# Operands in two parts for the next-state products of a state-space branch, and its B by C products taken for four token blocks at once, in a hybrid decoder trunk on one Trainium2 core

## The chip, the cores and the metric

The kernel runs on one core of one Trainium2 chip. The metric is device time in microseconds (us), the median of the runs. Lower is better. Engines are named as in the profile: PE is TensorE (matrix products, PEld its weight loads), DVE is VectorE, ACT is ScalarE, POOL is GpSimd, SP issues the loads and stores.

## The reference, cut to what matters

One decoder layer is computed for 512 tokens of width 1024 in float32: a norm, one wide projection, three mixing branches (dilated attention, pooling, a state-space branch), gates, an output projection, then a gated convolutional feed-forward part and a last norm. The change lies in the state-space branch, which goes over the tokens in four blocks of 128:

```python
xc = (x * dt[..., None]).reshape(b, c, l, g, e, p)
a_cs = jnp.cumsum(a, axis=-1)
Lmat = jnp.exp(jnp.where(causal, seg, -jnp.inf)).reshape(b, g, e, c, l, l)
cb = jnp.einsum("bclgn,bcsgn->bcgls", Cc, Bc)
y_diag = jnp.einsum("bcgls,bgecls,bcsgep->bclgep", cb, Lmat, xc)
decay = jnp.exp(a_cs[..., -1:] - a_cs).reshape(b, g, e, c, l)
states = jnp.einsum("bclgn,bgecl,bclgep->bcgepn", Bc, decay, xc)
def step(carry, inp):
    st, dec = inp
    return carry * dec[..., None, None] + st, carry
```

`y_off` takes C by the state carried into a block, and the branch's output is `y_diag + y_off`. There are two groups `g` of eight heads, a state of 128, and 64 channels a head.

## The kernel before, in words

**Stages.** The weights come in jobs of 256 columns or so. A job is loaded by SP (`raw`, in `fetch`), split by ScalarE into a high part in fp32r (`wh`, line 196) and by VectorE into the rest (`wl = raw - wh`, line 216), two jobs ahead of its use. TensorE then takes three fp32r products for each chunk (`mm3`, line 237): high by high, high by low, low by high. Each chunk collects in a PSUM bank (`pa`, `pqk`, `pu`, `pb`) and is then evacuated.

**The order of the work.** Each engine executes its instructions in the order in which the program writes them (`manual_schedule`). The big products follow a written list (`program`, `jobs`). The small work of attention and of the state-space branch stands in generators. After each chunk `step()` lets every running generator go on to its next `yield`; `ROWS`, `WHOLE` and `REST` order what they give TensorE within a step. So between two chunks of 24 long products (12, where `chunk_a2` halves a chunk) TensorE gets a few short ones.

**The state-space branch.** `ssd_start` queues `btok_item` for both groups, then `ssd_item(c, gi)` for block `c` and group `gi` in the order of `SSD_ORDER`, one new item at every other step. It runs beside the q and k products of the third attention group (`pqk`) and the gates (`pa`), from about 366 to 492 us.

- `btok_item` (lines 989 to 994) turns B (`XS[8 + gi]`) block by block with four transposes into the bank `pbt`, and ScalarE copies it to `btok`, in float32.
- `ssd_item` (lines 996 to 1071) first has SP load `al`, the cumulated decay spread over 128 partitions, and `ea`. It turns four blocks of x into `pxs` (line 1014); VectorE multiplies by dt into `xc` (1016). TensorE takes B by C of the block into `pcb` (line 1020), a plain float32 product of 128 columns, and VectorE masks it with a triangle into `cbt` (1022). GpSimd multiplies `xc` by the decay into `xd` (1025), for the first three blocks.
- One step on, VectorE subtracts in `al` head by head (1031) and ScalarE takes the exponentials (1032). One further, VectorE multiplies `al` by `cbt` (1036).
- Then comes the state: GpSimd scales the old one (1042), TensorE takes the product of `btok` and `xd` into `pst` (line 1045), a plain float32 product of 512 columns, and VectorE adds it (1050); in the first block ScalarE copies it (1048).
- Then `py` (1057, `xc` by `al`), `pyo` (1064, old state by C, four plain products), and VectorE's sums into the output (1066, 1067, 1070).

A plain float32 product appears in the trace as two records, an fp32r product as one.

**Buffers.** All the small PSUM banks (`SM`: `pbt`, `pxs`, `pcb`, `pst`, `py`, `pyo` and attention's `ps`, `pt`, `po`) share one ring of four, so each new one waits until an older one has been read. The SBUF tiles of `T` share a ring of 54. SP's queue is in order: weight loads, `al` and `ea` stand in it one behind the other.

Of the kernel before, what the change touches and what calls it, by code (L numbers as in the profile page):

```python
# [10 lines left out]
F32 = mybir.dt.float32  # L11
F32R = mybir.dt.float32r
AF = mybir.ActivationFunctionType
OP = mybir.AluOpType
AX = mybir.AxisListType

P = 128
# [66 lines left out]
def trunk(ctx: ExitStack, tc, out, x, rel_bias, ln1_g, w_in, b_gate, w_a, pool_w, pool_scale, w_b,  # L84
# [3 lines left out]
    act, dve, pool, pe, sp = nc.scalar, nc.vector, nc.gpsimd, nc.tensor, nc.sync  # L88
# [19 lines left out]
    def T(name, dt=F32, shape=(P, S)):  # L108
        return big.tile(list(shape), dt, name=name, tag="t")
# [4 lines left out]
    def SM(name):  # L114
        return psum.tile([P, S], F32, name=name, tag="sm")
# [5 lines left out]
    tri = cpool.tile([P, P], F32, name="tri")  # L121
# [27 lines left out]
    ROWS, WHOLE, REST = 1, 2, 3  # L149
# [744 lines left out]
    XS, YT, Y = {}, {}, {}  # L894
# [85 lines left out]
    def hb(t, c, h0, n=8):  # L980
        return t[:, c * SH + h0:c * SH + h0 + n].unsqueeze(2).to_broadcast([P, n, DH])

    def h3(t):
        return t.rearrange("p (h d) -> p h d", h=8)

    btok, prev, done = {}, {}, set()

    def btok_item(gi):
        yield WHOLE
        ps = SM("pbt")  # L990
        for c in range(4):
            pe.transpose(ps[:, c * P:(c + 1) * P], XS[8 + gi][:, c * P:(c + 1) * P], eye)
        t = btok[gi] = T("btok")
        act.copy(t, ps)

    def ssd_item(c, gi):
        cs = slice(c * P, (c + 1) * P)
        dtv, acs, dec, tot, ad, ed = (cst[n] for n in ("dtv", "acs", "dtz", "dts", "ad", "ed"))
        als = []
        for q in range(2):  # L1000
            al = T("al")
            h0 = 8 * gi + 4 * q
            sp.dma_start(al.rearrange("p (h l) -> p h l", h=4), ad[h0:h0 + 4, cs].partition_broadcast(P))
            als.append(al)
        if c:
            ea = T("ea")
            for i in range(2):
                h0 = 8 * gi + i
                sp.dma_start(ea[DH * i:DH * i + DH].rearrange("p (j l) -> p j l", j=4),
                             ed[h0:h0 + 8 - i:2, cs].partition_broadcast(DH))  # L1010
        yield WHOLE
        ps = SM("pxs")
        for j in range(4):
            pe.transpose(ps[:, j * P:(j + 1) * P], XS[4 * gi + j][:, cs], eye)
        xc = T("xc")
        dve.tensor_tensor(h3(xc), h3(ps), hb(dtv, c, 8 * gi), OP.mult)

        y = Y[gi][:, :, cs]
        pcb = SM("pcb")
        pe.matmul(pcb[:, :P], XS[8 + gi][:, cs], XS[10 + gi][:, cs], start=True, stop=True)  # L1020
        cbt = T("cbt", F32, (P, P))
        dve.tensor_tensor(cbt, pcb[:, :P], tri, OP.mult)
        if c < 3:
            xd = T("xd")
            pool.tensor_tensor(h3(xd), h3(xc), hb(dec, c, 8 * gi), OP.mult)  # L1025
        yield
        for q in range(2):
            a3 = als[q].rearrange("p (h l) -> p h l", h=4)
            for j in range(4):
                i = c * SH + 8 * gi + 4 * q + j  # L1030
                dve.tensor_scalar(a3[:, j, :], a3[:, j, :], acs[:, i:i + 1], 0.0, OP.subtract, OP.min)
            act.activation(als[q], als[q], AF.Exp)
        yield
        for q in range(2):
            a3 = als[q].rearrange("p (h l) -> p h l", h=4)
            dve.tensor_tensor(a3, a3, cbt.unsqueeze(1).to_broadcast([P, 4, P]), OP.mult)
        yield
        old = prev.get(gi)
        if c < 3:
            nw = T("st")  # L1040
            if c:
                pool.tensor_tensor(h3(nw), h3(old), hb(tot, c, 8 * gi), OP.mult)
            yield WHOLE
            pst = SM("pst")
            pe.matmul(pst, btok[gi][:, cs], xd, start=True, stop=True)
            yield REST
            if c == 0:
                act.copy(nw, pst)
            else:
                dve.tensor_tensor(nw, nw, pst, OP.add)  # L1050
            prev[gi] = nw
        yield
        py = SM("py")
        for j in range(4):
            for i in range(2):
                o, lo = (2 * j + i) * DH, (2 * j + i) % 4 * P
                pe.matmul(py[DH * i:DH * i + DH, j * P:(j + 1) * P], xc[:, o:o + DH],  # L1057
                          als[j // 2][:, lo:lo + P], start=True, stop=True)
        by_j = lambda t: t.rearrange("p (j l) -> p j l", j=4)
        yield WHOLE  # L1060
        if c:
            po = SM("pyo")
            for j in range(4):
                pe.matmul(po[:, j * P:(j + 1) * P], old[:, j * P:(j + 1) * P], XS[10 + gi][:, cs],
                          start=True, stop=True)
            dve.tensor_tensor(ea, po, ea, OP.mult)
            dve.tensor_tensor(ea, ea, py, OP.add)
        for j in range(4):
            m = 4 * gi + j
            dve.scalar_tensor_tensor(y[:, j, :], y[:, j, :], cst["dgc"][:, m:m + 1],  # L1070
                                     by_j(ea if c else py)[:, j, :], OP.mult, OP.add)
        done.add((c, gi))

    def ssd_start():
        for m in (8, 9, 0, 1, 2, 3, 10, 4, 5, 6, 7, 11):
            act.activation(XS[m], XS[m], AF.Silu)
        for gi in range(2):
            waiting.append(btok_item(gi))
        for c, gi, gap in SSD_ORDER:
            waiting.append(ssd_item(c, gi))  # L1080
            for _ in range(gap):
                waiting.append(FREE)
# [517 lines left out]
    for tb in (2, 3):  # L1600
        for h in range(2):
            t = xin[tb, h]
# [30 lines left out]
    n = 0  # L1633
# [67 lines left out]
```

## Time and profile before

| | |
|---|---|
| median of 3 runs | 1033.13 us (1032.23 to 1033.27) |
| the profiled execution: its own time | 1032.69 us |
| its span | 1030.9 us |
| TensorE busy | 1019.8 us, 5276 records |
| VectorE, ScalarE, GpSimd busy | 702.7, 490.2, 132.8 us |
| mean granted TensorE clock | 0.999 |

The time of an execution holds the span of its instructions and a little around it. Busy times of different engines lie beside one another. In the rows of a timeline the first figure is the start in us from the span's start, the second the stretch covered, then engine, line, operation, output and inputs by the program's names, shape and count; a bracket gives idle time before it and what ended it. Durations of neighbouring TensorE records overlap, so TensorE's cost is best read from start to start. In the table by stage, each engine's busy time stands with its number of instructions behind it, then the granted clock, the DMA engines' busy share and the rate moved.

### The profile page before, as it was taken

What the parts mean: (1) busy time and instruction counts of PE and PEld (TensorE: products, weight loads), DVE (VectorE), ACT (ScalarE), POOL (GpSimd) and SP (SyncE); (2) the same over time, 40 slices, a digit from 0 to 9 for tenths busy, and PEclk for the clock granted to TensorE, in tenths of its full rate; (3) what the DMA queues carried; (4) which work ended last, traced back from release to release, by engine and by line L of the source; (5) the groups of instructions that cost most, each with busy time, mean ns of one, the idle gap of its engine ahead of it and who ended that gap; (6) DMA issues with size and microseconds to landing.
All of it is one profiled execution on the core that took longest, in us unless ns stands there. A gap on an engine that the chain in (4) does not pass through costs nothing.

```text
span 1030.9 us, 13254 instructions
## 1 busy us (share of the span) xinstructions
PE 1019.8 (99%) x5276; PEld 858.0 (83%) x5276; DVE 702.7 (68%) x932; ACT 490.2 (48%) x784; POOL 132.8 (13%) x114
## 2 busy tenths in 40 slices
PE   8999999999999999999999999999999999999997
PEld 8998877899888887788888888898888888888885
DVE  6553566788756648666688856767778668685756
ACT  6432545454674363567575324545444434433434
POOL 1770000000000001100044501101111100111002
PEclk9999999999999999999999999999999999999999
DMA  8444312034322354551253625543232233421322
GB/s 270 135 129 137 108 57 75 31 88 138 123 82 82 93 158 108 133 144 44 80 151 128 203 82 203 171 142 121 82 122 83 84 117 112 138 82 41 123 82 82
DMA packets 113357, 117.62 MB, mean 114 GB/s; under 512 B 5236, under 2 KB 97207, under 8 KB 113296
## 3 DMA queue, kind: packets, MB, share of 16 engines
q1 hardware_dynamic: 112703, 115.92, 36.4%
q8 instruction: 41, 0.67, 0.3%
q10 hardware_dynamic: 592, 0.86, 0.2%
q14 instruction: 21, 0.16, 0.1%
HBM read 112.97 MB, written 2.22 MB: 112 GB/s over the span
## 4 chain that ended last, share of the span: by engine, by line
PE 91%; DVE 4%; ACT 3%; issue 1%; DMA 1%; ACTq 0%; DVEq 0%
PE pa L237 30%; PE pu L237 22%; PE pb L237 12%; PE pd L237 7%; PE pqk L237 6%; PE pa L1552 2%; PE pq L237 2%; PE pu L1356 1%; PE ps L743 1%; PE pt L772 1%; PE ppw L237 1%; PE po L784 1%; DVE xs L1133 1%; DVE wl L216 1%; PE py L1057 1%
## 5 line engine op out<-in xcount | busy, mean ns | idle before, releaser
L216 DVE TENSOR_TENSOR wl<-raw,wh 128x2048 fp32r<-128x2048 f32 (+3 forms) x95 | 220.3, 2320 | 53.3 <-ACT wh L196 43.5
L196 ACT CAST wh<-raw 128x1024 fp32r<-128x1024 f32 (+3 forms) x188 | 187.6, 1017 | 48.3 <-DVE raw L341 18.0
L1251 DVE SCALAR_TENSOR_TENSOR hc<-pu,fcol,hc 128x510 f32<-128x510 f32 x88 | 65.8, 748 | 56.0 <-ACT hc L1248 54.4
L237 PE MATMUL pa<-uh,wh 128*128 128x512 f32 x384 | 98.4, 398 | 0.0
L237 PE MATMUL pa<-ul,wh 128*128 128x512 f32 x384 | 94.9, 389 | 0.0
L237 PE MATMUL pa<-uh,wl 128*128 128x512 f32 x384 | 94.8, 389 | 0.0
L237 PEld LDWEIGHTS pa<-ul,wh 128*128 128x128 f32 x384 | 72.1, 188 | 15.1
L237 PEld LDWEIGHTS pa<-uh,wl 128*128 128x128 f32 x384 | 72.1, 188 | 15.0
L237 PE MATMUL pu<-uh,wh 128*128 128x512 f32 (+1 forms) x352 | 83.6, 379 | 0.0
L237 PE MATMUL pu<-uh,wl 128*128 128x512 f32 (+1 forms) x352 | 83.5, 379 | 0.0
L237 PE MATMUL pu<-ul,wh 128*128 128x512 f32 (+1 forms) x352 | 83.5, 379 | 0.0
L237 PEld LDWEIGHTS pa<-uh,wh 128*128 128x128 f32 x384 | 70.3, 188 | 14.8 <-issue 1.0
L237 PEld LDWEIGHTS pu<-ul,wh 128*128 128x128 f32 x352 | 64.2, 188 | 12.5
L237 PEld LDWEIGHTS pu<-uh,wl 128*128 128x128 f32 x352 | 64.2, 188 | 12.5
L237 PEld LDWEIGHTS pu<-uh,wh 128*128 128x128 f32 x352 | 64.1, 188 | 12.4
L1248 ACT ACTIVATE hc<-pu,fcol,fcol 128x512 f32<-128x512 f32 x40 | 31.2, 780 | 80.5 <-PE pu L237 80.5
L1256 POOL TENSOR_TENSOR hc<-hc 128x512 f32<-128x512 f32 x22 | 30.8, 1402 | 289.1 <-DVE hc L1251 252.0
L1025 POOL TENSOR_TENSOR xd<-xc,dtz 128x512 f32<-128x512 f32 x6 | 6.4, 1063 | 355.9 <-issue 307.5
L765 ACT ACTIVATE sb<-sb,nmls 128x128 f32<-128x128 f32 (+1 forms) x72 | 30.1, 419 | 30.4 <-DVE nmls L762 17.7
L1149 ACT ACTIVATE sg<-pa,col 128x512 f32<-128x512 f32 x24 | 16.5, 688 | 45.5 <-PE pa L237 45.4
L1253 ACT ACTIVATE hc<-hc 128x512 f32<-128x512 f32 x22 | 13.9, 632 | 39.9 <-DVE hc L1251 39.9
L907 DVE SCALAR_TENSOR_TENSOR xs<-pa,col,xs 128x509 f32<-128x509 f32 (+2 forms) x24 | 18.0, 749 | 18.7 <-ACT xs L903 18.2
(373 smaller groups left out, 1868.0 us busy)
## 6 DMA issues: line engine op xcount, KB each, us to landing
raw<-in_w_in_dram SPq DMA_DIRECT2D x25, 1024.0 KB, 5.5
raw<-in_ffn_w_up_dram SPq DMA_DIRECT2D x22, 1024.0 KB, 5.2
raw<-in_w_o_dram SPq DMA_DIRECT2D x8, 1024.0 KB, 6.6
raw<-in_ffn_w_down_dram SPq DMA_DIRECT2D x8, 1024.0 KB
raw<-in_w_in_dram SPq DMA_DIRECT2D x14, 512.0 KB, 3.9
raw<-in_w_in_dram SPq DMA_DIRECT2D x6, 768.0 KB
raw<-in_w_b_dram SPq DMA_DIRECT2D x4, 1024.0 KB, 5.2
al<-ad SPq DMA_DIRECT2D x16, 256.0 KB, 7.7
```

Source lines behind the costliest of these rows:

```text
L196: act.copy(job.high[:, :, o], job.raw[:, :, o])
L216: (eng or dve).tensor_tensor(l[:, :, o], job.raw[:, :, o], h[:, :, o].bitcast(F32), OP.subtract)
L237: pe.matmul(ps, l, r, start=first and n == 0, stop=last and n == total - 1, skip_group_check=onto)
L743: pe.matmul(pss[i][:, o:o + w * P], q[r, n * P:(n + 1) * P], k[r, kb * P:(kb + w) * P], start=True, stop=True)
L765: act.activation(sb[:, off:off + w * P], sb[:, off:off + w * P], AF.Exp, bias=nm[:, n, h:h + 1], accum_out=ls[:, n, h:h + 1])
L907: dve.scalar_tensor_tensor(t[:, sh:], ps[:, :S - sh], col[:, o_cw + 12 * k + m:o_cw + 12 * k + m + 1], t[:, sh:], OP.mult, OP.add)
L1149: act.activation(s, ps, AF.Sigmoid, bias=col[:, o:o + 1])
L1248: act.activation(t, ps, AF.Identity, bias=ff["c1"][:, ff["b"] + m:ff["b"] + m + 1], scale=fw(2, m))
L1251: dve.scalar_tensor_tensor(t[:, sh:], ps[:, :S - sh], fw(k, m), t[:, sh:], OP.mult, OP.add)
L1253: act.activation(t, t, AF.Silu)
L1256: pool.tensor_tensor(a, a, t, OP.mult)
L1552: pe.matmul(first[2 * n + j][:, lo:hi], a[:, k, j * P:(j + 1) * P], b[:, k, lo:hi], start=a is wh and b is uh and k == 0, stop=a is wl and ...
```

## The change

`btok_item` keeps turned B in two parts: ScalarE's copy into fp32r (`bth`) and VectorE's difference (`btl`). After one more step it also takes B by C for all four blocks into one bank, and VectorE masks them in one instruction; `ssd_item` reads its block's slice. In `ssd_item` the decayed `xd` is multiplied by VectorE in place of GpSimd, ScalarE casts it to fp32r (`xdh`), and VectorE takes the difference (`xdl`) behind the subtractions of the next step. The state's product becomes three fp32r products of the parts, collected in the same bank.

```diff
     def btok_item(gi):
         yield WHOLE
         ps = SM("pbt")
         for c in range(4):
             pe.transpose(ps[:, c * P:(c + 1) * P], XS[8 + gi][:, c * P:(c + 1) * P], eye)
-        t = btok[gi] = T("btok")
-        act.copy(t, ps)
+        h, l = btok[gi] = T("bth", F32R), T("btl", F32R)
+        act.copy(h, ps)
+        dve.tensor_sub(l, ps, h.bitcast(F32))
+        yield
+
+        yield WHOLE
+        ps = SM("pcb")
+        for c in range(4):
+            cs = slice(c * P, (c + 1) * P)
+            pe.matmul(ps[:, cs], XS[8 + gi][:, cs], XS[10 + gi][:, cs], start=True, stop=True)
+        t = cbt[gi] = T("cbt")
+        four = lambda t: t.rearrange("p (c l) -> p c l", c=4)
+        dve.tensor_tensor(four(t), four(ps), tri.unsqueeze(1).to_broadcast([P, 4, P]), OP.mult)
...
         y = Y[gi][:, :, cs]
-        pcb = SM("pcb")
-        pe.matmul(pcb[:, :P], XS[8 + gi][:, cs], XS[10 + gi][:, cs], start=True, stop=True)
-        cbt = T("cbt", F32, (P, P))
-        dve.tensor_tensor(cbt, pcb[:, :P], tri, OP.mult)
         if c < 3:
             xd = T("xd")
-            pool.tensor_tensor(h3(xd), h3(xc), hb(dec, c, 8 * gi), OP.mult)
+            dve.tensor_tensor(h3(xd), h3(xc), hb(dec, c, 8 * gi), OP.mult)
+            xh, xl = T("xdh", F32R), T("xdl", F32R)
+            act.copy(xh, xd)
         yield
...
             act.activation(als[q], als[q], AF.Exp)
+        if c < 3:
+            dve.tensor_sub(xl, xd, xh.bitcast(F32))
         yield
         for q in range(2):
             a3 = als[q].rearrange("p (h l) -> p h l", h=4)
-            dve.tensor_tensor(a3, a3, cbt.unsqueeze(1).to_broadcast([P, 4, P]), OP.mult)
+            dve.tensor_tensor(a3, a3, cbt[gi][:, cs].unsqueeze(1).to_broadcast([P, 4, P]), OP.mult)
...
             pst = SM("pst")
-            pe.matmul(pst, btok[gi][:, cs], xd, start=True, stop=True)
+            bh, bl = btok[gi]
+            for n, (b, t) in enumerate(((bh, xh), (bh, xl), (bl, xh))):
+                pe.matmul(pst, b[:, cs], t, start=n == 0, stop=n == 2)
```

In the changed program's order, the group of four B by C products of the first group stands just ahead of the turning of the second B, and that of the second group just ahead of the first turning of x. The number of loads, of table loads and of steps stays as it was.

More of the change, by code (lines that the diff above doesn't have):

```diff
@@ L984, in h3 @@
         return t.rearrange("p (h d) -> p h d", h=8)
-    btok, prev, done = {}, {}, set()
+    btok, cbt, prev, done = {}, {}, {}, set()
     def btok_item(gi):
```

## The prediction

> **What bounds the kernel now.** The page comes first: busy shares, then the chain that ended last.
>
> ```profile
> PE 1019.8 (99%) x5276; PEld 858.0 (83%) x5276; DVE 702.7 (68%) x932; ACT 490.2 (48%) x784; POOL 132.8 (13%) x114
> PE 91%; DVE 4%; ACT 3%; issue 1%; DMA 1%; ACTq 0%; DVEq 0%
> ```
>
> TensorE works 99% of the 1030.9 us span and makes 91% of the chain. A term counts only if it shortens or lengthens TensorE's own sequence, or if it makes TensorE wait. The second view is the table by stage, around the state-space branch that the change touches.
>
> ```profile
> core 0: us, PE busy (x) PEld busy (x) DVE busy (x) ACT busy (x) POOL busy (x), PEclk, DMA share, GB/s
> ...
> 380.00:400.00 20.00, 20.00 (x106) 15.43 (x106) 16.31 (x41) 9.46 (x13) 3.93 (x4) 1.00 0.72 199
> 400.00:420.00 20.00, 20.00 (x130) 16.05 (x126) 13.40 (x35) 5.57 (x8) 3.09 (x3) 1.00 0.38 101
> ```
>
> TensorE is full in both stretches, VectorE is at 16.31 of 20 us in the tightest, and the granted clock is 1.00. So I price TensorE's terms from start to start on its timeline (durations there overlap), and then ask whether VectorE's added work is ever late.
>
> **TensorE, the state product (six times).**
>
> ```profile
> 405.16 1.02 PE L1045 MATMUL pst<-xd,btok 128*128 128x512 f32 x2
> ...
> 407.87 1.98 PE L237 MATMUL pa<-ul,wh 128*128 128x512 f32 x8
> 409.69 1.98 PE L237 MATMUL pa<-uh,wl 128*128 128x512 f32 x8
> ...
> 435.29 1.02 PE L1045 MATMUL pst<-xd,btok 128*128 128x512 f32 x2
> 436.14 0.60 PE L772 MATMUL pt<-eye,sb 128*128 128x128 f32 x4
> ```
>
> Eight fp32r products of 512 columns take 409.69 - 407.87 = 1.82 us, 0.227 each. The plain product takes 407.87 - 405.16 - 1.82 = 0.89 us where fp32r products follow, and 436.14 - 435.29 = 0.85 where a turning follows. By the changed program's order three fp32r products of the same shape stand in its place: 3 x 0.227 = 0.68. Three of the six are followed by fp32r products and save 0.21, three stand next to plain fp32 work and save 0.17 to 0.18: together **-1.16 us**, with 6 x 0.17 = 1.02 and 6 x 0.21 = 1.26 as ends. The Trainium skill ("FP8 and Floating Point Precision", TensorE Precision Notes) says that true FP32 makes four passes through the array. Counting it as four passes against three at 0.227 would give 6 x 0.227 = 1.36 us, so -2.05 us in all instead of the sum below; the rows show a plain product a little cheaper than four fp32r ones, and I go by the rows.
>
> **TensorE, B by C (eight products in place, now two groups of four).**
>
> ```profile
> 369.10 0.60 PE L992 MATMUL pbt<-eye,xcv 128*128 128x128 f32 x4
> ...
> 371.39 1.99 PE L237 MATMUL pqk<-ul,wh 128*128 128x512 f32 x8
> ...
> 400.75 1.16 PE L1064 MATMUL pyo<-xcv,st 128*128 128x128 f32 x8
> 401.74 0.60 PE L1014 MATMUL pxs<-eye,xs 128*128 128x128 f32 x4
> 402.18 0.39 PE L1020 MATMUL pcb<-xcv 128*128 128x128 f32 x2
> ...
> 403.33 1.08 PE L237 MATMUL pqk<-ul,wh 128*128 128x512 f32 x4
> ...
> 428.53 0.60 PE L1014 MATMUL pxs<-eye,xs 128*128 128x128 f32 x4
> 429.48 0.49 PE L1020 MATMUL pcb<-xcv 128*128 128x128 f32 x2 [0.35 <-DVE ea L1066]
> ...
> 431.66 1.98 PE L237 MATMUL pa<-ul,wh 128*128 128x512 f32 x8
> ...
> 460.68 0.66 PE L1014 MATMUL pxs<-eye,xs 128*128 128x128 f32 x4
> 461.37 0.49 PE L1020 MATMUL pcb<-xcv 128*128 128x128 f32 x2
> ...
> 463.54 1.98 PE L237 MATMUL pa<-ul,wh 128*128 128x512 f32 x8
> ```
>
> Four turnings alone cost 371.39 - 369.10 - 1.82 = 0.47 us (eight fp32r products stand in the gap); turnings plus one pcb cost 403.33 - 401.74 - 0.91 = 0.68 (four in the gap). So one pcb in place costs 0.21, eight 1.68. Twice it costs more: 431.66 - 428.53 - 1.82 = 1.31 and 463.54 - 460.68 - 1.82 = 1.04, that is 0.63 and 0.36 above 0.68. The bracket names the reason: pcb needs a PSUM bank that VectorE's `ea` has just to read, right behind pyo. Removed in all: 1.68 + 0.99 = 2.67 us.
>
> Added: two groups of four plain 128-column products with four different weights. That form is in the trace: pyo, 401.74 - 400.75 = 0.99 us. Two cost 1.98; the bounds are 4 x 0.21 = 0.84 and 0.99 each, and I take the row of the same form. Net **-0.69 us** (-0.99 at the low end). The bank wait has no new place on TensorE's path: in the changed order pyo is followed by the turnings and then by 12 or 24 long products (2.7 or 5.5 us), and the next bank that `ea` must give back goes to the state product or the turnings behind them.
>
> Sum: -1.16 - 0.69 = **-1.85 us**, if nothing else makes TensorE wait.
>
> **The added work off TensorE.** ScalarE gets six casts, VectorE six `xd`, six `xdl`, two `btl`, two `cbt` of 512 columns for eight of 128; GpSimd loses six `xd`. Rows for the durations and for the moments that decide:
>
> ```profile
> 378.86 0.69 DVE L1016 TENSOR_TENSOR xc<-pxs,dtv 128x512 f32<-128x512 f32 x1 [0.44 <-PE pxs L1014]
> 379.47 0.28 DVE L1022 TENSOR_TENSOR cbt<-pcb,tri 128x128 f32<-128x128 f32 x1
> 379.67 2.52 DVE L1031 TENSOR_SCALAR al<-al,acs 128x128 f32<-128x128 f32 x8
> 385.33 1.30 DVE L1036 TENSOR_TENSOR al<-al,cbt 128x512 f32<-128x512 f32 x2 [3.14 <-ACT al L1032]
> 388.58 1.65 DVE L1031 TENSOR_SCALAR al<-al,acs 128x128 f32<-128x128 f32 x8
> 392.35 1.29 DVE L1036 TENSOR_TENSOR al<-al,cbt 128x512 f32<-128x512 f32 x2
> ```
>
> ```profile
> 391.50 1.09 PE L1057 MATMUL py<-al,xc 128*64 128x128 f32 x16
> 399.72 1.09 PE L1057 MATMUL py<-al,xc 128*64 128x128 f32 x16
> ```
>
> ```profile
> 379.69 1.05 POOL L1025 TENSOR_TENSOR xd<-xc,dtz 128x512 f32<-128x512 f32 x1 [307.46 <-issue]
> ```
>
> A VectorE pass over 128x512 takes 0.69 us (xc has xd's very form). The first `py` starts 4.9 us after its `al` (391.50 against 386.63), the second 6.1 us after (399.72 against 393.64). Ahead of the first now stand two btl, two cbt, one xd and one xdl, 6 x 0.69 = 4.1, less one old cbt 0.28 and less 0.87: the eight subtractions took 2.52 us beside GpSimd's `xd` and 1.65 without it, and GpSimd's `xd` is gone. That is 3.0 us. TensorE itself arrives later there: two groups of four less two single ones, 1.98 - 0.42 = 1.56, less one state product's 0.21. So even if none of VectorE's 3.14 us idle took anything up, 4.9 + 1.35 - 3.0 = **3.2 us** are left. Ahead of the second `py` come xd, xdl and one old cbt less, 1.1 us more: 6.1 + 0.9 - 4.1 = 2.9 us. The later `py` have 24 long products (5.5 us) ahead of them in place of 12, so I take their margins as wider. The first state product also waits for `xdl`: the subtractions ended at 379.67 + 2.52 = 382.2, so xdl ends at 382.2 + 3.0 = 385.2, and TensorE gets there 12 long products, itself and the step into `py` (2.7 + 0.7 + 0.1) ahead of 391.50 + 1.35, near 389.3. I cost all this at nothing; without that cover each us of lateness costs one us. The bounds are 0 and +5.5 us (second rival).
>
> The Trainium skill ("SBUF — State Buffer", Who interferes with whom) says that a VectorE instruction with two SBUF inputs contends with a GpSimd one that reads SBUF, and that `tensor_scalar` can do so in its 2-port mode. The 2.52 us against 1.65 agree for `tensor_scalar`; by that rule VectorE gets part of its added time back, which changes no term on TensorE.
>
> The queues that hang on VectorE and ScalarE:
>
> ```profile
> SPq L184 <- DVE wl L216: 136.9, 12, 14.1
> 392.50 0.38 SPq L184 DMA_DIRECT2D raw<-in_w_in_dram  x1
> 392.93 1.12 SPq L1003 DMA_DIRECT2D al<-ad  x2
> 394.15 1.79 SPq L1009 DMA_DIRECT2D ea<-ed  x2
> al<-ad SPq DMA_DIRECT2D x16, 256.0 KB, 7.7
> 405.96 1.75 DVE L1031 TENSOR_SCALAR al<-al,acs 128x128 f32<-128x128 f32 x8
> 413.63 1.04 ACT L196 CAST wh<-raw 128x1024 fp32r<-128x1024 f32 x1
> ```
>
> SP's weight loads wait for VectorE's `wl`, which slips here by at most the 4.1 us of added work, and the `al` and `ea` loads stand behind them in order. The load of 392.50 is cast at 413.63. The `al` of 392.93 lands 7.7 us after its issue, near 401.7, and is first used at 405.96, itself later then. The `ea` of 394.15 is the one read before 429.48. So none is late enough to hold TensorE. ScalarE's six casts (an estimate of 0.7 us each, as VectorE's passes) stand where it is busy 9.46 and 5.57 of 20 us, and GpSimd's six `xd` lay beside TensorE's work: both at nothing.
>
> Own time of the profiled execution: 1032.69 (span 1030.9 and 1.8 around it). 1032.69 - 1.85 = 1030.84. The median of the runs is 1033.13, which would give 1031.28; I predict **1031.1**, between them.
>
> **The rivals.**
>
> *The bank wait comes back.* The 0.99 us of stalls in front of pcb may reappear in front of the turnings or the state product, which take the same ring of four banks. For it: the ring stays, and VectorE is busier. Against: the covers of 2.7 and 5.5 us. Then -1.16 - 0.69 + 0.99 = -0.86 us: 1032.0. That is also the case in which the grouping does not do what it says: four in a row cost 0.99 against 4 x 0.21.
>
> *VectorE becomes late (slower).* Place: the second `py`, near 400 us. It could happen if the new instructions took what such subtractions take elsewhere, beside GpSimd:
>
> ```profile
> 542.23 3.48 DVE L1140 TENSOR_TENSOR ytl<-xs,yth 128x512 fp32r<-128x512 f32 x2
> ```
>
> 1.74 us each instead of 0.69. Eight new ones stand ahead of that `py` (two btl, two cbt, two xd, two xdl): 8 x 1.05 = 8.4 us more, against 2.9 to spare. TensorE would wait 5.5 us: 1032.69 - 1.85 + 5.5 = 1036.3. Point: from 2.9 us of unpriced work on TensorE waits, and from 2.9 + 1.85 = 4.8 on the kernel is slower. Against: GpSimd is nearly idle there once `xd` has left it, and VectorE's idle of 3.14 us is counted as of no use.
>
> *More comes free.* Both low ends hold: groups of four at 0.84 us, as the single pcb would have it, and 0.21 saved at each of the six state products. -1.26 - 0.99 = -2.25: 1030.4. For it: the first product of a group already pays the step from fp32r to plain float32. Against: pyo is the same form and took 0.99.
>
> **How the numbers follow.** Forecast (1030.5 to 1031.7) 0.55; bank wait back 0.20; more comes free 0.17; VectorE late 0.08. The range 1030.0 to 1032.7 takes in the first three with half a us for the spread of the runs, and leaves out the last. 0.2% is 2.07 us, about what a measurement of this kernel can tell from no change: the forecast lies at 0.18%, so it falls mostly under no difference. Faster: 0.17 and a third of the forecast, 0.35; slower 0.08; same 0.57.
>
> **What would show it.** The profile after should have three fp32r rows for pst with starts 0.23 apart, turnings followed directly by pa at 0.47, no wait of TensorE for `ea`, two pcb groups of about 1 us before 381 us, `py` never waiting for `al` or `xdl`, and `al` subtractions near 1.65 us everywhere. A TensorE wait for VectorE between 385 and 402 us would prove the forecast wrong, as would pst steps above 0.8 us.

## The result and the profile after

| | before | after |
|---|---|---|
| median of 20 runs each | 1033.16 us (1032.23 to 1034.94) | 1031.16 us (1030.78 to 1032.49) |
| ratio after to before, 95% interval | | 0.9982 (0.9975 to 0.9988) |
| profiled execution, own time and span | 1032.69, 1030.9 us | 1031.29, 1029.5 us |

The forecast was 1031.1 us in a range of 1030.0 to 1032.7. The time fell by 2.00 us, 0.19%, and came out 0.06 us from the forecast. The sum behind it sized one term 0.20 us too small and left out a wait that took back 0.76 us in the profiled execution, so the parts are worth more than the total.

The page of the kernel after, busy time by engine and the chain that ended last:

```profile
PE 1018.4 (99%) x5282; PEld 859.5 (83%) x5282; DVE 709.0 (69%) x940; ACT 494.1 (48%) x790; POOL 129.2 (13%) x108
PE 90%; DVE 5%; ACT 3%; DMA 1%; issue 1%; ACTq 0%; DVEq 0%
```

TensorE still bounds the kernel and has lost 1.4 us of work; VectorE has 6.3 us more, ScalarE 3.9. TensorE's timeline in the kernel after, at the places that the change touches:

```profile
369.10 0.60 PE L992 MATMUL pbt<-eye,xcv 128*128 128x128 f32 x4
...
375.03 1.05 PE L1002 MATMUL pcb<-xcv 128*128 128x128 f32 x8
375.92 0.60 PE L992 MATMUL pbt<-eye,xcv 128*128 128x128 f32 x4
379.13 1.05 PE L1002 MATMUL pcb<-xcv 128*128 128x128 f32 x8
380.02 0.60 PE L1025 MATMUL pxs<-eye,xs 128*128 128x128 f32 x4
...
405.61 0.39 PE L1058 MATMUL pst<-xdh,bth 128*128 128x512 f32 x1
405.84 0.39 PE L1058 MATMUL pst<-xdl,bth 128*128 128x512 f32 x1
406.07 0.39 PE L1058 MATMUL pst<-xdh,btl 128*128 128x512 f32 x1
406.29 1.98 PE L237 MATMUL pa<-uh,wh 128*128 128x512 f32 x8
...
428.37 0.60 PE L1025 MATMUL pxs<-eye,xs 128*128 128x128 f32 x4
428.73 2.08 PE L237 MATMUL pa<-uh,wh 128*128 128x512 f32 x8
...
458.03 1.16 PE L1077 MATMUL pyo<-xcv,st 128*128 128x128 f32 x8
460.04 0.66 PE L1025 MATMUL pxs<-eye,xs 128*128 128x128 f32 x4 [0.86 <-ACT o L790]
...
503.13 0.61 PE L797 MATMUL pst<-eye,nmls 128*38 128x128 f32 x4
```

Read from start to start: a group of four takes 375.92 - 375.03 = 0.89 us, the second too (380.02 - 379.13). The three fp32r products take 406.29 - 405.61 = 0.68. The turnings at 428.37 are followed at once by the long products, without the stall for `ea` of before. New in its size is the bracket at 460.04: TensorE waits for ScalarE's copy of `o` (the last attention group's output, line 790), which reads the PSUM bank of `po`; the turnings of the last block need that bank. From `pyo` to these turnings it is now 2.01 us; before it was 460.68 - 459.43 = 1.25, and 0.99 where nothing holds them. So a wait of 0.25 us has become one of 1.0. The 0.25 is the copy itself: before, it starts as soon as `po` is finished (459.54), takes 1.09 us and ends 0.05 us ahead of the turnings.

The last row is the turning of attention's statistics, by which the branch is over. I use it as a clock. What lies ahead of the branch is the same code in all kernels here, but it ended anywhere from 369.10 to 371.83 us in their profiled executions; the stretch from the first turning of B (`pbt`) to this row leaves that out. Before, the rows of `pyo` and of this turning are

```profile
459.43 1.16 PE L1064 MATMUL pyo<-xcv,st 128*128 128x128 f32 x8
...
504.47 0.62 PE L797 MATMUL pst<-eye,nmls 128*38 128x128 f32 x4
```

and the stretch is 504.47 - 369.10 = 135.37 us. After, `pbt` starts at 369.10 as well, and the stretch is 134.03: 1.34 us shorter.

### The profile page after: what moved, and what is told of

It reads as the page before. It is cut to its first block, busy times and chain, and to the rows that moved or that the text cites. A ratio compares the mean times of both kernels' runs of the same rounds, so it can differ in the third digit from the quotient of the medians.

```text
span 1029.5 us, 13279 instructions
## 1 busy us (share of the span) xinstructions
PE 1018.4 (99%) x5282; PEld 859.5 (83%) x5282; DVE 709.0 (69%) x940; ACT 494.1 (48%) x790; POOL 129.2 (13%) x108
## 4 chain that ended last, share of the span: by engine, by line
PE 90%; DVE 5%; ACT 3%; DMA 1%; issue 1%; ACTq 0%; DVEq 0%
PE pa L237 29%; PE pu L237 22%; PE pb L237 12%; PE pd L237 7%; PE pqk L237 6%; PE pa L1565 2%; PE pq L237 2%; PE pu L1369 1%; PE ps L743 1%; PE pt L772 1%; PE ppw L237 1%; PE po L784 1%; DMA al<-ad 1%; DVE xs L1146 1%; DVE wl L216 1%
## 5 line engine op out<-in xcount | busy, mean ns | idle before, releaser
L1053 POOL TENSOR_TENSOR st<-st,dts 128x512 f32<-128x512 f32 x4 | 6.8, 1707 | 381.2 <-ACT st L1061 320.7
```

## The experiments

The theory after the result: the change's own terms on TensorE are -1.16 us (state product) and -0.89 us (B by C), and a wait for the copy of `o` gives some of it back in some executions. The rivals: the gain comes from something else that moved (GpSimd's `xd`, the order on VectorE), or one half does all of it. All diffs are against the kernel after, if nothing else is said. The times of all runs stand in one table at the end of this section.

**1. The grouping alone.** B by C in groups of four, the state product in one plain part as before, `xd` on GpSimd:

```diff
-            for n, (b, t) in enumerate(((bh, xh), (bh, xl), (bl, xh))):
-                pe.matmul(pst, b[:, cs], t, start=n == 0, stop=n == 2)
+            pe.matmul(pst, btok[gi][:, cs], xd, start=True, stop=True)
```

> Only B by C in groups of four; the state product stays plain, xd stays on GpSimd. My theory (TensorE's own terms add up): two groups at 0.89 us replace eight single products of 0.21 and 0.99 us of bank waits, so the attention statistics' turning near 503 us comes 0.9 us earlier than before if the turnings of the last block still wait for the copy of o only 0.25 us; VectorE carries no xd or xdl here, so that wait should not grow. Median 1032.3, ratio 0.9991. Rival (the gain is the state product's alone): no change, ratio 1.000.

Measured: 1033.36 us against 1033.37 before, ratio 1.0001 (0.9992 to 1.001). The groups cost 0.89 and 0.88 us and the stalls for `ea` are gone, so the own term is there, but the stretch is 135.38 us, as before. TensorE's timeline in this run shows where it went, and ScalarE's shows why:

```profile
461.74 1.16 PE L1070 MATMUL pyo<-xcv,st 128*128 128x128 f32 x8
463.93 0.66 PE L1024 MATMUL pxs<-eye,xs 128*128 128x128 f32 x4 [1.03 <-ACT o L790]
```

```profile
459.99 1.28 ACT L1155 ACT_TABLE_LOAD   x1 [1.08 <-PE pa L237]
461.28 0.69 ACT L1155 ACTIVATE sg<-pa,col 128x512 f32<-128x512 f32 x1
461.87 1.03 ACT L196 CAST wh<-raw 128x1024 fp32r<-128x1024 f32 x1
462.80 1.07 ACT L790 COPY o<-po 128x512 f32<-128x512 f32 x1
```

The gap from `pyo` to the turnings is 463.93 - 461.74 = 2.19 us, a wait of 1.20 where it was 0.25: +0.95 against -0.89. In this program the table load ahead of `sg` waits for TensorE's chunk `pa`, which only `sg` reads. Before, the load ran while the chunk was still being computed:

```profile
456.61 1.28 ACT L1149 ACT_TABLE_LOAD   x1
457.91 0.69 ACT L1149 ACTIVATE sg<-pa,col 128x512 f32<-128x512 f32 x1
458.49 1.03 ACT L196 CAST wh<-raw 128x1024 fp32r<-128x1024 f32 x1
459.54 1.09 ACT L790 COPY o<-po 128x512 f32<-128x512 f32 x1
```

There `sg` starts 0.38 us after `py` (457.53), here 1.44 us after it (459.84). So the time is the rival's, but not for its reason. By the traces the wait goes with the built program: the program of experiment 10, which differs from this one in the engine of the copies of `o` alone, has it at the same three places, and the kernel before, which has such a wait at 411.75 us (2.85 us), keeps it there under the same edit (experiment 9). Why the built programs differ in it stays open, and with one trace of each it isn't proved that it never varies.

**2. The parts alone.** B by C in place, the state product in three parts:

```diff
+        pcb = SM("pcb")
+        pe.matmul(pcb[:, :P], XS[8 + gi][:, cs], XS[10 + gi][:, cs], start=True, stop=True)
+        cbt = T("cbt", F32, (P, P))
+        dve.tensor_tensor(cbt, pcb[:, :P], tri, OP.mult)
```

> Only the state product in parts, with xd and xdl on VectorE; B by C stays block by block. My theory: six state products save 0.17 to 0.21 us each, 1.16 together; the two bank waits in front of pcb stay (about 1 us), and the wait for the copy of o may grow by up to 0.8 us since VectorE's chain is later: 0.4 to 1.2 us earlier at the statistics, median 1032.0 to 1032.8. Rival (parts give nothing, a plain product costs no more than three fp32r ones): 0 or later.

Measured: 1032.73 us, ratio 0.9991 (0.9982 to 0.9999). The state product's slots are 0.68 us, the stall of 0.35 us for `ea` in the third block is still there, and the table load has the wait of experiment 1, with TensorE held 1.05 us by `o`. The stretch is 134.87: -0.50 where the slots alone give -1.16. So both halves shorten TensorE's sequence as priced, and both lose to the same place.

**3. `xdl` one step later**, behind VectorE's multiplications of `al`:

```diff
-        if c < 3:
-            dve.tensor_sub(xl, xd, xh.bitcast(F32))
         yield
         for q in range(2):
...
+        if c < 3:
+            dve.tensor_sub(xl, xd, xh.bitcast(F32))
```

> The changed kernel with xdl taken one step later, behind the product of al and cbt. Theory A (in the changed kernel the last block's turnings wait 0.86 us for ScalarE's copy of o, which is late because xdl stands ahead of attention's sums on VectorE): that wait shrinks by about 0.6 us, the statistics' turning comes at 502.5 instead of 503.1. Theory B (the late load of al makes the copy of o late): the subtractions hold VectorE just as long, nothing changes. Median 1030.6 by A, 1031.2 by B.

Measured: 1032.57 us, ratio 0.999 (0.9981 to 0.9999), 0.80 us below the kernel before where the change is 2.00 below it. Neither text came out as written: the wait for `o` went (the gap from `pyo` is 1.28 us, but TensorE also gets there later), and another came, here on TensorE's timeline of this run:

```profile
406.09 0.40 PE L1058 MATMUL pst<-xdh,bth 128*128 128x512 f32 x1
407.71 0.50 PE L1058 MATMUL pst<-xdl,bth 128*128 128x512 f32 x1 [1.22 <-DVE xdl L1047]
```

The second part comes 1.62 us behind the first instead of 0.23, so +1.39; with -2.05 that is -0.66, and the stretch of 134.85 says -0.52. Where `xdl` stands on VectorE does matter: the place that the change gives it is early enough, one step on is not.

**4. The copy of `o` on VectorE** for the last attention group (three copies), which takes ScalarE's table load, `sg` and cast out of the bank's way:

```diff
-                act.copy(blocked(o, g), grouped(po, g))
+                (dve.tensor_copy if g == 2 else act.copy)(blocked(o, g), grouped(po, g))
```

> The changed kernel with the third attention group's copy of o on VectorE in place of ScalarE. By theory A and B alike the wait is in ScalarE's queue (exponentials, a table load, a sigmoid and a cast stand ahead of the copy); VectorE is idle before 459.2 us, so the copy would end near 459.4 and the turnings wait 0.3 us less than 0.86 or not at all: 0.5 to 0.8 us earlier, median 1030.5. Rival (the wait is on the product po itself): nothing changes.

Measured: **1030.24 us** (1030.03 to 1030.39), ratio 0.9964 (0.9952 to 0.9977), below both kernels. TensorE's timeline in this run:

```profile
458.35 1.16 PE L1077 MATMUL pyo<-xcv,st 128*128 128x128 f32 x8
459.60 0.66 PE L1025 MATMUL pxs<-eye,xs 128*128 128x128 f32 x4
```

The gap is back at 1.25 us, and the stretch is 133.32: -2.05 against before, which is -1.16 - 0.89 to the hundredth. This run alone doesn't show that the edit brought the gap back: ScalarE's cast ends at 458.51 here, so its copy could have run as early as VectorE's did (458.47), and experiment 6 has the same stretch with the copy on ScalarE. What the edit does to the wait is seen in experiments 1 and 10.

A second gain lies behind the branch, and it is most of what the edit brings here: from the turning of the statistics to the end of the span it takes 525.46 us instead of 526.37. TensorE's wait for `al` (line 846, the attention output's low part) is gone, 0.6 us by its bracket in the kernel after and 0.88 from start to start. The traces show how. The third copy of `o` now stands on VectorE ahead of attention's statistics, so these come later (505.01 us instead of 503.78), and so do GpSimd's products `o<-o,wb` (line 835), at 535.74 instead of 535.07. In the kernel after, a pair of VectorE's multiplications (`xs`, line 1146, from 535.78) lies wholly beside them and takes 3.48 us. Here the pair starts at 535.28, ahead of them, and takes 2.45. VectorE then reaches its last `al` at 564.05 instead of 565.58. All nine kernels with the copy on ScalarE show 3.48 to 3.49 us there and this wait; all five with it on VectorE show 2.44 to 2.45 and no such wait.

**5. Two of the three parts.** The kernel leaves out the product of B's low part by `xd`'s high part, so its state is less exact:

```diff
-            for n, (b, t) in enumerate(((bh, xh), (bh, xl), (bl, xh))):
+            for n, (b, t) in enumerate(((bh, xh), (bh, xl))):
```

> The changed kernel without the third product of the parts (low of B by high of xd); the output leaves out that small term. My theory (TensorE's own sequence is the time): six products of 0.227 us fewer, 1.36 us less at the statistics' turning, unless the wait for the copy of o eats some: median 1029.8 to 1030.4. Rival (TensorE's time there is covered by something else): nothing.

Measured: 1030.73 us, ratio 0.997 (0.9959 to 0.9981); the stretch is 132.87, 1.16 shorter than after. Six products fewer at 0.227 would be 1.36; this program too has the table load that waits, and its wait for `o` is 0.18 us longer, which is the rest. The median is 0.33 us above the expected range and 2.37 below the kernel before, only 0.37 more than the change's 2.00. That fits if most runs of the change lack the wait that its profiled execution has.

**6. `xd` back on GpSimd**, all else as in the change:

```diff
-            dve.tensor_tensor(h3(xd), h3(xc), hb(dec, c, 8 * gi), OP.mult)
+            pool.tensor_tensor(h3(xd), h3(xc), hb(dec, c, 8 * gi), OP.mult)
```

> The changed kernel with xd back on GpSimd, cast and difference as they are. Theory: xd takes 1.05 us on GpSimd, the eight subtractions of al beside it take 2.5 us again in place of 1.65 in the blocks where they overlap; VectorE gains 0.69 a block and loses up to 0.9, so margins stay about the same and TensorE's own terms are untouched: ratio to before 0.998 as for the changed kernel, statistics' turning within 0.5 us of 503.1. Rival (moving xd to VectorE is what made the gain): back to 504.4.

Measured: 1031.12 us, ratio 0.9982 (0.9972 to 0.9991), the same as the change. In the profiled execution the gap from `pyo` to the turnings is 1.25 us, and the stretch is 133.33. So the move of `xd` brings nothing by itself. The trace also shows what the wait for `o` hangs on. VectorE's timeline of this run, and then of the kernel after, at the same block:

```profile
447.29 1.26 DVE L1040 TENSOR_SCALAR al<-al,acs 128x128 f32<-128x128 f32 x4 [0.54 <-DMA al<-ad]
449.44 0.87 DVE L1040 TENSOR_SCALAR al<-al,acs 128x128 f32<-128x128 f32 x4 [0.89 <-DMA al<-ad]
450.23 0.68 DVE L1043 TENSOR_TENSOR xdl<-xd,xdh 128x512 fp32r<-128x512 f32 x1
451.03 0.69 DVE L758 SCALAR_TENSOR_TENSOR sb<-ps,b 128x512 f32<-128x512 f32 x1
```

```profile
450.53 1.68 DVE L1040 TENSOR_SCALAR al<-al,acs 128x128 f32<-128x128 f32 x8 [3.42 <-DMA al<-ad]
452.12 0.68 DVE L1043 TENSOR_TENSOR xdl<-xd,xdh 128x512 fp32r<-128x512 f32 x1
452.92 0.69 DVE L758 SCALAR_TENSOR_TENSOR sb<-ps,b 128x512 f32<-128x512 f32 x1
```

ScalarE's timeline of the kernel after, the chain from there to the copy:

```profile
454.43 0.40 ACT L765 ACTIVATE sb<-sb,nmls 128x128 f32<-128x128 f32 x1 [0.72 <-DVE nmls L762]
...
456.10 1.28 ACT L1162 ACT_TABLE_LOAD   x1
457.39 0.69 ACT L1162 ACTIVATE sg<-pa,col 128x512 f32<-128x512 f32 x1
457.98 1.03 ACT L196 CAST wh<-raw 128x1024 fp32r<-128x1024 f32 x1
458.91 1.08 ACT L790 COPY o<-po 128x512 f32<-128x512 f32 x1
```

`al` was issued at nearly the same moment in both, at 441.37 us in the kernel after and 441.30 here. VectorE began to subtract in it 9.2 us later in the kernel after and 6.0 here, where the second half followed at 8.1; the subtractions end 1.9 us apart. In the kernel after it is late; attention's scores (`sb`, line 758) stand behind `al` on VectorE, ScalarE's exponentials wait for them (0.72), and its table load, `sg`, cast and copy follow without a gap. The copy then ends at 459.99, and the turnings start at 460.04. TensorE is no earlier there: `pyo` starts 88.93 us after `pbt` in both. What makes the load late was not separated.

**7 and 8. VectorE's margin ahead of the second `py`.** Five, and then twelve, subtractions that nobody reads, behind `xdl` of one block:

```diff
+        if (c, gi) == (1, 0):
+            junk = T("junkv")
+            for _ in range(5):
+                dve.tensor_sub(junk, xd, xh.bitcast(F32))
```

> The changed kernel with five idle subtractions of 128x512 more on VectorE behind xdl of the second block, 3.0 to 3.4 us. Theory: the second py has 4.7 us to spare, so it starts where it does now, 400.4, within 0.1 us. Rival (VectorE is already the limit there): the second py starts 3 us later.

> The same with twelve idle subtractions, 7.2 to 8.2 us. Theory: past the 4.7 us to spare TensorE waits for al in front of the second py by 2.5 to 3.5 us, and most of it stays in the total. Rival (VectorE never holds TensorE there): nothing; rival (it holds already): 7 us or more.

Measured, one run each: 1031.48 and 1038.10 us, stretches 133.32 and 139.95. Five take 4.32 us and cost nothing; `al` is ready at 400.85 and TensorE takes it up at 401.31. Twelve take 9.41 where 7.2 to 8.2 were expected, the wait is 4.11 where 2.5 to 3.5 were, and TensorE's timeline in that run reads

```profile
405.51 1.98 PE L1074 MATMUL py<-al,xc 128*64 128x128 f32 x16 [4.11 <-DVE al L1051]
407.41 2.08 PE L1081 MATMUL pyo<-xcv,st 128*128 128x128 f32 x8
```

`py` takes 1.90 us from start to start instead of 1.0. The table by stage of the same run has the reason in its granted clock (the third figure from the right):

```profile
401.00:405.50 4.50, 0.40 (x2) 0.03 (x1) 4.43 (x6) 0.00 (x0) 0.00 (x0) 0.81 0.00 0
405.50:409.30 3.80, 3.79 (x25) 3.47 (x26) 3.77 (x13) 0.89 (x2) 0.00 (x0) 0.50 0.91 288
409.30:412.00 2.70, 2.70 (x12) 2.34 (x11) 2.70 (x8) 2.21 (x4) 0.00 (x0) 0.75 0.89 171
412.00:416.00 4.00, 4.00 (x19) 3.32 (x18) 3.90 (x9) 0.00 (x0) 0.00 (x0) 1.00 0.46 111
```

After 4.1 us without work TensorE ran at half its clock for 3.8 us and at a mean of 0.75 over the next 2.7: 3.8 x 0.5 + 2.7 x 0.25 = 2.6 us lost. The stretch grew by 139.95 - 133.32 = 6.6, the wait and this. In finer windows the granted clock falls near 403.9, 2.5 us after the end of the last product's record, and is back at 1.00 near 410.7, 5.1 us after the work began again. The Trainium skill ("TensorE: Matmul & The Clock Gate", Part 1: The HAM clock gate) says that the clock falls to half after an idle window of some 3.4 us and returns after as long a busy one, and that these windows run freely. This run agrees on the fall to half and on the return, but the clock fell before TensorE had been idle for a whole such window, and the return took longer than one.

**9 to 12. The same copy of `o` on VectorE in four kernels**, to see each half of the change without ScalarE's copy in the way: the kernel before, the grouping alone, the parts alone, and the change with `xd` on GpSimd, each with the edit of experiment 4.

> The kernel before, with the third attention group's copy of o on VectorE. Theory (the copy of o on ScalarE is a separate brake, there before the change too): the 0.25 us wait of the last block's turnings of x goes, and so does TensorE's wait for al behind the span's last stage, worth 1.0 us in the run of the changed kernel with this edit; 1.2 us below the kernel before, the stretch from the first turning of B to the turning of the statistics at 135.1 us instead of 135.37. Rival (the copy is a brake only where the change has brought TensorE there earlier): stretch 135.4 us, time within 0.3 us of the kernel before.

> B by C in groups of four, state product in one plain part, copy of o on VectorE. Theory (with the wait for o out of the way each half of the change brings its own terms): 0.90 us below the run of the kernel before with the same edit of o (groups of four at 0.89 against 1.68 and 0.99 of stalls), stretch 134.2 us. Rival (the grouping only moves its stall, as in the first run of it): the same time as that kernel within 0.3 us, with a wait at another PSUM bank of 0.6 us or more.

> State product in three fp32r parts, B by C in place, copy of o on VectorE. Theory: 1.16 us below the run of the kernel before with the same edit of o, stretch 134.0 us, the stall of 0.35 us for ea at the third block still there. Rival (the two halves don't add up, part of the 2.05 us comes only from both together): 0.5 us or less.

> The changed kernel with the copy of o on VectorE and the decayed xd back on GpSimd. Theory (the move of xd is worth nothing, since VectorE's work lies beside TensorE's): 1030.2 us, stretch 133.3 us, as with the edit of o alone. Rival (VectorE's time counts): 0.5 us or more away from that, on either side.

Measured: 1035.56 us with a ratio of 1.0019 (1.001 to 1.0028); 1031.43, 0.9983 (0.9974 to 0.9992); 1032.33, 0.999 (0.9981 to 0.9998); 1030.41, 0.997 (0.9958 to 0.9983). The first missed both texts: the kernel before gets slower. Its timeline of TensorE, then of VectorE:

```profile
460.82 0.66 PE L1014 MATMUL pxs<-eye,xs 128*128 128x128 f32 x4
463.38 0.49 PE L1020 MATMUL pcb<-xcv 128*128 128x128 f32 x2 [1.91 <-DVE ea L1066]
```

```profile
459.69 1.08 DVE L790 COPY o<-po 128x512 f32<-128x512 f32 x1 [4.37 <-PE po L784]
460.61 2.12 DVE L1036 TENSOR_TENSOR al<-al,cbt 128x512 f32<-128x512 f32 x2
462.65 0.68 DVE L1066 TENSOR_TENSOR ea<-pyo,ea 128x512 f32<-128x512 f32 x1
```

With B by C in place, `pcb` needs `pyo`'s bank back at once. VectorE reads that bank in `ea`, which now stands behind the copy of `o` and the multiplications behind it, so what ScalarE no longer holds, VectorE holds longer. The parts alone have the same stall, 1.05 us. With the grouping no `pcb` stands there, and the edit gains. The clean pair is experiment 1 and experiment 10: the table load waits at the same place in both (1.08 and 1.09 us), the gap from `pyo` falls from 2.19 to 1.32 us, and the stretch is 0.90 shorter. The copy of `o` is thus no brake of its own, as my theory had it: whether moving it pays inside the branch depends on the grouping.

Experiments 10 and 11 missed their texts with it, since these start from experiment 9: the runs lie 4.13 and 3.23 us below it where 0.90 and 1.16 were expected, with stretches of 134.48 and 135.32 where 134.2 and 134.0 were. Experiment 12 came out as its theory has it.

All of them in one table. The stretch is of the profiled execution, its difference is to before, and the last column is the median less that of the kernel before on the same chip (after: the 20 runs):

| kernel | `o` on ScalarE: stretch | difference | median | `o` on VectorE: stretch | difference | median |
|---|---|---|---|---|---|---|
| before | 135.37 | 0 | 0 | 137.24 | +1.87 | +2.15 |
| grouping alone | 135.38 | +0.01 | -0.01 | 134.48 | -0.89 | -1.98 |
| parts alone | 134.87 | -0.50 | -0.64 | 135.32 | -0.05 | -1.08 |
| the change | 134.03 | -1.34 | -2.00 | 133.32 | -2.05 | -3.13 |
| the change, `xd` on GpSimd | 133.33 | -2.04 | -1.98 | 133.30 | -2.07 | -3.00 |

On the right, what lies behind the branch is 0.5 to 1.0 us shorter in each kernel, so those medians lie below the stretches' differences (the run of the kernel before with the edit is the fastest of its 11, so its stretch is a low one). From the grouping to the change the right half gives 134.48 - 133.32 = 1.16 us. From one `py` to the next, it comes as 0.23 us at each of the first three state products and 0.14 to 0.17 at each of the other three, with 0.07 of the last a wait (the gaps of 1.32 and 1.25): 1.09 to 1.16 for the six.

## Why the prediction was right, and where it was not

- **TensorE is the bound, and terms count from start to start: right.** Every difference above is a slot or a wait on TensorE's timeline.
- **State product, -1.16: right.** The slots are 0.68 as priced, and the table gives 1.09 to 1.16 between two kernels that differ in little else. The count of four passes would have given 0.227 for each product. Three of the six gave 0.23, which fits it, and three less, so its 1.36 is too large in sum. That its total, -2.05, is the one that came is chance: B by C made up the difference.
- **B by C, -0.69: the mechanism right, a term mis-sized.** "That form is in the trace: pyo, 0.99 us": a group took 0.89, not 0.99, so the term is -0.89. The low bound of 0.84 was nearer. What `pyo` holds in the other 0.10 us was not separated.
- **"The bank wait has no new place on TensorE's path": half wrong.** It is right for `ea`, which holds TensorE nowhere in the kernel after. But the step looked only at the banks that VectorE reads. The turnings of the last block take the bank of `po`, which ScalarE reads, and already waited 0.25 us for it; in the profiled execution ScalarE came late and TensorE waited 1.0. In experiments 6 and 7 TensorE gets there just as early and the wait is 0.25. The first rival (the stall in front of the turnings) thus came true in part, with another releaser: it takes back 0.76 us, -2.05 + 0.76 = -1.29 against -1.34 measured.
- **The `al` load, "none is late enough to hold TensorE": wrong by way of two engines.** A load whose subtractions end 1.9 us later reaches TensorE through VectorE's scores and ScalarE's copy. Experiments 6 and 7, where `al` was used earlier, show no such wait. The change's median (-2.00) is nearer to its own terms (-2.05) than to its profiled execution (-1.34). Experiment 4 lowers the median by 1.13 us, and 0.91 of that lies behind the branch in the traces, so some 0.2 us (an estimate) are left for this wait in a typical run, not 0.76. That most runs of the change lack it fits, but is only argued, since runs without a profile don't show it.
- **VectorE's margin: right, and too small.** 2.9 us at the second `py` were counted; 4.32 us of idle work fitted in. In the kernel after, `al` is ready at 395.73, 2.1 us later than before where 4.1 were counted, and TensorE takes it up at 400.42, so there are 4.7. VectorE's idle time, which the prediction had counted as of no use, is what could take up the rest. The second rival did not occur.
- **"Without that cover each us of lateness costs one us": wrong** for long waits. A wait of 4.1 us cost 6.6, because of the clock.
- **GpSimd's `xd` at nothing: right** (medians of -1.98 against -2.00, and with the copy of `o` on VectorE stretches of 133.30 against 133.32).
- **The total.** The forecast of 1031.1 came from own terms that were 0.20 us too small, from an offset between profiled execution and median that was split in the middle, and from no wait for `o`. The first two nearly cancel, and the third hardly shows in the median. Its nearness is partly luck.

## What to carry to other kernels

Where TensorE is full, price a change by start-to-start slots of the same form in the same company, and then look, for each PSUM bank of a shared ring that TensorE will now reach earlier, who reads it last and what stands ahead of that read on its engine. A saved slot is kept only if the next bank is free earlier too: alone the grouping shortened the stretch by nothing, and with the copy of `o` moved out of the way by 0.89 us. An edit that frees a bank on one engine is to be tried together with the edits that take waiting readers off the other, since the same edit made the kernel before 2.2 us slower. And look where a gain lies before you explain it: the change with the copy moved gave 3.1 us instead of 2.0, and most of the difference came from another place, where VectorE got ahead of GpSimd.

## What the runs showed of the hardware that was not expected

- A table load on ScalarE can carry the wait of the activation behind it: ahead of the copy of `o` it waited 1.08 us in experiments 1 and 2 and 1.09 in 5 for a TensorE result that only the activation reads, and what stood behind it came about 1 us later.
- One wait of 4.1 us on TensorE brought a granted clock of 0.50 over the next 5.1 us of its work.
- Four plain products of 128 columns cost 0.89 us as a group between long fp32r products and turnings, and 0.99 as `pyo`, behind `py`.
- The load of `al` took 6.0 to 9.2 us from issue to its first use, at the same place of nearly the same program.
- A pair of VectorE multiplications took 2.45 us when it started ahead of GpSimd's products and 3.48 wholly beside them, and a later wait of TensorE, 0.88 us from start to start, came with the second and not with the first.
